# Two projections 512 columns wide, and layer 0's modulation multiplied unsplit in four column groups

## The chip, the cores and the metric

The kernel runs on one core of one Trainium2 chip. The metric is the device time of one execution in microseconds (us): the median of three runs is 1244.5 (1243.15 to 1247.92). The profile shows one execution more, with a span of 1242.4 us. Its engines are TensorE (PE; PEld is its weight load), VectorE (DVE), ScalarE (ACT), GpSimd (POOL) and SyncE (SP), which issues the loads.

## The reference

Two layers act on 512 prompt tokens and 256 sample tokens, which share the weights and have a modulation vector `c` each. The model width is 1024. For each layer:

```python
mod = jax.nn.silu(c) @ w_ada + b_ada
shift, scale, gate = jnp.split(mod, 3, axis=-1)
hid = _rms_norm(x, norm_g) * (1.0 + scale[:, None, :]) + shift[:, None, :]
qa, ka, va, za, qb, kb, vb, zb, ga, gb = jnp.split(hid @ w_in, split_at, axis=-1)
oa = _neighbourhood_attention(qa, ka, va, rpb)
qh = _axial_rope(_rms_norm(qb, q_norm_g))
kh = _axial_rope(_rms_norm(kb, k_norm_g))
ob = _gqa_attention(qh, kh, vb)
merged = sigmoid(ga) * ((oa * silu(za)) @ w_pa) + sigmoid(gb) * ((ob * silu(zb)) @ w_pb)
x = x + gate[:, None, :] * (merged @ w_out)
```

A final RMS norm ends the trunk. `va` are the values of the neighbourhood attention, `qb` the queries of the grouped attention; both are 512 columns wide and come from the same input `hid`.

## The kernel before, in words

**Numbers.** Every factor of a large product is held as a high and a low part in a rounded 32-bit format (fp32r), and a product is three: high x high, high x low, low x high. A weight of 128x1024 elements (512 KB, "half" or "unit") is loaded on SP into one of two buffers (`raw`, `w_load`), ScalarE rounds it (`whi`, L243), and VectorE, for five halves GpSimd, subtracts (`wlo`, L249). When `wlo` has been issued, `w_load` issues the next load but one, which waits on SP until its buffer is free; what stands behind it on SP waits too.

**Order.** All instructions are issued from one program in an order written out by hand. Main work is a list of steps (`step`), mostly of twelve products. Attention work comes as slots between the steps at a rate, and other pieces follow a number of steps later (`defer`). Each engine runs its instructions in the order of this program. At the start the order comes from a table instead: `put(t, fn)` with a written time `t`, sorted by it; `load` computes the times of the loads from their number and a cost `U`.

**The start.** The first work is the norm of the prompt's rows of x and layer 0's modulation. Sections 1 (scale) and 0 (shift) come as 16 quarters of 256 KB each (`adaraw`). A quarter is split by ScalarE (`adahi`) and by VectorE or GpSimd (`adalo`, L1051), three quarters stay unsplit; the matmuls `adap` multiply it with the silu of `c`, once for each group of tokens. Four quarters give 256 columns: `rows` copies the sums to SBUF, two small matmuls `adat` turn them into columns, and VectorE adds the bias to `ada_shift` or `ada_a`. From there come the eight parts k of the layer's input: VectorE multiplies x by `ada_a` and the norm `rb` (L285), ScalarE adds the shift and rounds (`hh`, L293), VectorE subtracts (`hl`, L299). Then va is multiplied: two chunks of 256 columns, the prompt's four token tiles of the first chunk with k outermost (each k starts when its `hh` and `hl` are there), then the second chunk, then the sample's two tiles, whose norm is computed meanwhile (`ssq`, `ssps`, `ms`, `ny`, `rb`). `acct` names these sums. Behind va come the "pairs" (`accp` for the prompt's 512 tokens, `accs` for the sample's 256): queries and keys of two heads, with the neighbourhood attention of the pair before in slots (`tp` transposes, `pth` and `ptl` copies in two parts, `op` and `os` products with the values).

**qb.** Two chunks of 256 columns, three sums of two token tiles each. Each sum is squared and copied by ScalarE (`rsq`, `rr`), reduced by VectorE (`qss`), and GpSimd multiplies by the rotary tables. When a chunk's three sums are through, `rope_finish` computes the reciprocal root of all 24 norms in twelve small VectorE operations and multiplies the three `rr` by it (L1314); TensorE transposes them (`qt`), ScalarE and VectorE copy these out (`GQ`). The chunk kvb and the slots of the last pair follow in the same way.

Of the kernel before, what the change touches and what calls it, by code (L numbers as in the profile page):

```python
# [7 lines left out]
F32 = mybir.dt.float32  # L8
# [17 lines left out]
    # the first loads: order of the quarters (section, chunk), where the rows of x and the first weights come in,  # L26
    # how early a load is issued, which engine takes the low part of a quarter (R: the quarter stays whole)
    ORD=((1, 0), (0, 0), (1, 1), (0, 1), (1, 2), (0, 2), (1, 3), (0, 3)),
    XB=0,
    XS=1,  # L30
    WAT=(9, 20),
    LA=7,
    PL0="VVGVGGGVVVRVGVVV",
    PL1="VRGGGVRVGVGVGVGV",
    GL=1.8,
    # the first products: allowances between the pieces of a quarter, a chunk and the layer's input
    ML0=0.5,
    ML1=0.5,
    RL0=0.5,
    RL1=1,  # L40
    FL=0.6,
    HL=1.5,
    PL=0.7,
    # the first norm: which engine adds a square (P: the tensor engine), allowances; products that keep the array's clock up
# [3 lines left out]
    WARM=(10, 1, 22, 0.73),  # L48
    CH=4,
    # pieces at which the next weights are split, and halves whose low part GpSimd takes  # L50
    AK0=(2, 5),
    AK1=(3, 5),
    PW=("wor01", "wor11", "va11"),
    # neighbourhood attention: steps before a pair's slots start, steps for 16 slots; steps for what is left of it
# [3 lines left out]
    # grouped attention: steps before its norms, transposes and slots, steps for the slots  # L58
    QF=6,
    QT=11,  # L60
    QTT=3,
# [4 lines left out]
    # the other modulation sections: steps for the slots, loads ahead, slots before the sums are added up  # L66
# [4 lines left out]
    # steps before the prompt's next input, and before its result  # L71
# [7 lines left out]
def trunk(ctx: ExitStack, tc: tile.TileContext, xT, wst, wad, wsd, vec, gain, trig, mask, eye, rpb, yT):  # L79
# [23 lines left out]
    cst = const.tile([128, 160], F32R, name="cst")  # L103
# [110 lines left out]

    chunk_of = {}
# [11 lines left out]
    def split_one(now=True):  # L227
        low_all()
        if done_split[0] >= len(splits):
            return  # L230
        name, k = splits[done_split[0]]
        i = done_split[0]
        w_load(i + 1)
        if k == 0:
            wts[name] = (
                wp.tile([128, 8, 256], F32R, tag="whi", name="whi"),
                wp.tile([128, 8, 256], F32R, tag="wlo", name="wlo"),
            )
        hi, lo = wts[name]
        r = raws.pop(i)  # L240
        rv = r.rearrange("p (k n) -> p k n", k=4)
        h = hi[:, 4 * k:4 * k + 4, :]
        A.activation(out=h, in_=rv, func=AF.Copy)  # L243
        done_split[0] += 1

        def low():
            key = f"{name[0]}{name[2] if len(name) > 2 else ''}{k}"
            eng = G if key in SC["PW"] and (name[1] or name[0] != "va") else V
            eng.tensor_sub(out=lo[:, 4 * k:4 * k + 4, :], in0=rv, in1=h.bitcast(F32))  # L249
            w_load(i + 3)  # L250

        lows.append(low)
        if now:
            low_all()
# [13 lines left out]
    def ahead(name, at):  # L268
# [35 lines left out]
    def hid_chain(l, g, xs):  # L304
        """Pieces that turn the finished rows of group g into the two parts of the layer's input."""
# [115 lines left out]
    def ada_rows(acc):  # L421
        rows = smp.tile([4, 256], F32, tag="rows", name="rows", bufs=1)
        A.activation(out=rows, in_=acc[0:4, :], func=AF.Copy)
        return rows

    def ada_col(rows):
        pt = ps_t.tile([128, 2, 2], F32, tag="t", name="adat")
        for m in range(2):
            mm(pt[:, m, :], rows[:, 128 * m:128 * m + 128], sel[0:4, :], m == 0, m == 1)
# [86 lines left out]
    def token_chunk(name, evac, banks=(0, 1, 2), kouter=False, keep=False, more=True):  # L516
        if not kouter:
            need_split(name)
        hi, lo = wts[name]
        if not keep:  # L520
            wts.pop(name)

        def mms(out, i, k, st):
            hh, hl = hid[i // 4, k]
            i = i % 4
            sl = slice(128 * i, 128 * i + 128)
            mm(out, hh[:, sl], hi[:, k, :], st, False)
            mm(out, hh[:, sl], lo[:, k, :], False, False)
            mm(out, hl[:, sl], hi[:, k, :], False, k == KC - 1)

        if kouter:
            accs = {b: ps_acc.tile([128, 2, 256], F32, tag="acc", name="acct") for b in banks}

            def piece(k):
                for b in banks:
                    for j in range(2):
                        mms(accs[b][:, j, :], 2 * b + j, k, k == 0 and j == 0)
                    if k == KC - 1:
                        evac(b, accs[b])
                if more and k in SC["AK1" if name[1] else "AK0"]:  # L540
                    ahead(name, k)

            return [lambda k=k: piece(k) for k in range(KC)]
        cur = {}
        for b in banks:
            for j in range(4):
                def f(b=b, j=j):
                    if j == 0:
                        cur[b] = ps_acc.tile([128, 2, 256], F32, tag="acc", name="acct")
                    i = 2 * b + j // 2  # L550
                    for k in range(4 * (j % 2), 4 * (j % 2) + 4):
                        mms(cur[b][:, j // 2, :], i, k, k == 0 and j == 0)
                    if j == 3:
                        defer(2, lambda: evac(b, cur[b]))
                    if more and (b == banks[0] and j == 2 or b == banks[1 % len(banks)] and j == (1 if len(banks) > 1 else 3)):
                        ahead(name, j)
                step(f)

    def feat_chunk(name, src, nk, evac, ksteps=2, groups=(0, 1), keep=False, sep=False):
        need_split(name)  # L560
        hi, lo = wts[name]
        if not keep:
            wts.pop(name)
# [3 lines left out]
        def mms(out, m, g, k, st):  # L567
# [3 lines left out]
            else:  # L571
                xh, xl = src[k]
                sl = slice(0, NP) if g == 0 else slice(NP, NT)
            ms = slice(128 * m, 128 * m + 128)
            mm(out, hi[:, k, ms], xh[:, sl], st, False)
            mm(out, hi[:, k, ms], xl[:, sl], False, False)
            mm(out, lo[:, k, ms], xh[:, sl], False, k == nk - 1)

        cnt = [0]
        for g in groups:  # L580
            for m in range(2):
                kk = per * (1 + g)
                for k0 in range(0, nk, kk):
                    def f(g=g, m=m, k0=k0, kk=kk):
                        if k0 == 0:
# [19 lines left out]
                        if not (keep and name[2] == 3) and cnt[0] in ((3, 6) if len(groups) == 2 else (3, 5) if groups[0] == 0 else (2, 3)):  # L605
                            ahead(name, k0)
                    step(f)

    v4s = {}

    def va_evac(l, i):
        nxt(("va", l, i))
        cell = {}

        def evv(b, acc):
            if not cell:
                cell[0] = vp.tile([128, 6, 4, 128], F32R, tag="v", name="v4")
                v4s[i] = cell[0]
            evac_v(cell[0], b, acc)
        return evv  # L620

    def evac_v(v4, b, acc):
        tiles = slice(2 * b, 2 * b + 2)
        vv = v4[:, tiles].rearrange("p t (r e) (u d) -> p (t r) (e u) d", e=2, u=2)
        base = v4[:, tiles]
        off = base.offset
        pp = pitch(base)
        hi_o = bass.AP(base.tensor, off, [pp, [256, 4], [192, 2], [1, 64]])
        lo_o = bass.AP(base.tensor, off + 64, [pp, [256, 4], [64, 2], [1, 64]])
        src = acc.rearrange("p t (r e d) -> p (t r) e d", e=2, d=64)  # L630
        A.activation(out=hi_o, in_=src, func=AF.Copy)
        defer(1, lambda: V.tensor_sub(out=lo_o, in0=src, in1=hi_o.bitcast(F32)))
# [340 lines left out]
    order = []  # L973
    for l in range(DEPTH):
        order += [("va", l, 0), ("va", l, 1)]
        order += [("pair", l, p) for p in range(4)]
        order += [("qb", l, 0), ("qb", l, 1), ("kvb", l)]
# [7 lines left out]
    for nm in order:  # L985
        plan_chunk(nm, 1 if nm[0] in ("pa", "pb") else 2)
# [6 lines left out]
    with tc.manual_schedule():  # L993
# [3 lines left out]
        V.memset(cst.bitcast(F32), 0.0)  # L997
        xs, x_s = x_tiles("x0")
# [5 lines left out]
        c4 = cst[:, 0:32].rearrange("p (k f) -> p k f", f=4)  # L1004
        csv = cs.rearrange("p (k g) -> p k g", g=2)
        V.tensor_copy(out=c4[:, :, 0:2], in_=csv)
        V.tensor_sub(out=c4[:, :, 2:4], in0=csv, in1=c4[:, :, 0:2].bitcast(F32))
# [3 lines left out]
        V.tensor_add(out=sel, in0=ident[:, 0:2], in1=ident[:, 2:4])  # L1011
# [14 lines left out]
        U = 0.73  # L1026
# [11 lines left out]
        def q_load(sec, k):  # L1038
            raw = galloc([128, 2, 256], F32, "adaraw")
            S.dma_start(out=raw, in_=wad[sec, k])  # L1040
            quarter[sec, k] = [raw]

        def q_hi(sec, k):
            h = galloc([128, 2, 256], F32R, "adahi")
            A.activation(out=h, in_=quarter[sec, k][0], func=AF.Copy)
            quarter[sec, k].append(h)

# [737 lines left out]
```

## Time and profile before

| what | us |
|---|---|
| median of three runs | 1244.5 |
| span of the profiled execution | 1242.4 |
| TensorE busy | 1217.4 (98%) |
| VectorE busy | 827.2 (67%) |
| ScalarE busy | 596.3 (48%) |
| GpSimd busy | 377.5 (30%) |
| first product of va starts | 27.25 |
| first product of a pair starts | 77.63 |
| va of layer 1: the last 204 products start | 652.36 |

Times in a view of the trace count from the start of the span. A row of the groups has the line, engine and operation, then out<-in, shapes and the count; behind the first bar the busy time in all and the mean of one in ns; behind the second the idle time ahead of them and what ended it. A row of a timeline has start, length, engine, line, names. Matmuls are pipelined: a product of 256 columns has a length of 0.28 us, though the next starts 0.12 us after it. A row of the windows has the stretch, its length, the busy time (and number) for PE, PEld, DVE, ACT and POOL, then the clock granted to TensorE (1.00 is full), the share of the DMA engines that was busy, and GB/s.

### The profile page before, as it was taken

What the parts mean: (1) busy time and instruction counts of PE and PEld (TensorE: products, weight loads), DVE (VectorE), ACT (ScalarE), POOL (GpSimd) and SP (SyncE); (2) the same over time, 40 slices, a digit from 0 to 9 for tenths busy, and PEclk for the clock granted to TensorE, in tenths of its full rate; (3) what the DMA queues carried; (4) which work ended last, traced back from release to release, by engine and by line L of the source; (5) the groups of instructions that cost most, each with busy time, mean ns of one, the idle gap of its engine ahead of it and who ended that gap; (6) DMA issues with size and microseconds to landing.
All of it is one profiled execution on the core that took longest, in us unless ns stands there. A gap on an engine that the chain in (4) does not pass through costs nothing.

```text
span 1242.4 us, 20757 instructions
## 1 busy us (share of the span) xinstructions
PE 1217.4 (98%) x7872; PEld 1099.6 (89%) x7872; DVE 827.2 (67%) x1610; ACT 596.3 (48%) x1246; POOL 377.5 (30%) x396
## 2 busy tenths in 40 slices
PE   8999999999999999999999999999999999999996
PEld 7999999989898988887899999998988998888886
DVE  6857787784556458998384678878556544773535
ACT  6546865555555432333243676655555542232323
POOL 5114446352222121111050354554322212211102
PEclk9999999999999999999999999999999999999998
DMA  9432331110011134555352333112011103331324
GB/s 356 132 108 74 91 108 35 64 41 34 34 52 51 55 105 143 173 178 192 127 181 72 91 94 91 52 52 69 18 52 52 47 22 103 121 116 52 127 94 153
DMA packets 48852, 118.38 MB, mean 95 GB/s; under 512 B 5488, under 2 KB 13040, under 8 KB 48752
## 3 DMA queue, kind: packets, MB, share of 16 engines
q1 hardware_dynamic: 48608, 116.98, 29.3%
q8 instruction: 62, 1.02, 0.3%
q14 instruction: 38, 0.31, 0.1%
q10 hardware_dynamic: 144, 0.07, 0.0%
HBM read 110.74 MB, written 6.29 MB: 94 GB/s over the span
## 4 chain that ended last, share of the span: by engine, by line
PE 77%; DVE 11%; ACT 3%; issue 3%; DMA 3%; POOL 2%; SPq 1%; DVEq 0%; ACTq 0%; POOLq 0%
PE accp L132 35%; PE accs L132 16%; PE acct L132 11%; DVE adaacc L455 4%; PE go L132 3%; PE gtp L918 3%; PE gsp L132 3%; DVE wlo L249 2%; DMA adaraw<-in_wad 2%; PE sp L132 1%; PE op L132 1%; ACT p L756 1%; PE tp L777 1%; POOL gp L907 1%; DVE adalo L464 1%
## 5 line engine op out<-in xcount | busy, mean ns | idle before, releaser
L132 PE MATMUL accp<-hh,whi 128*128 128x512 f32 x512 | 202.9, 396 | 0.0
L132 PE MATMUL accp<-hh,wlo 128*128 128x512 f32 x512 | 200.2, 391 | 2.1 <-DVE wlo L249 2.1
L132 PE MATMUL accp<-hl,whi 128*128 128x512 f32 x512 | 200.0, 391 | 0.0
L249 DVE TENSOR_TENSOR wlo<-raw,whi 128x1024 fp32r<-128x1024 f32 x119 | 158.0, 1329 | 8.6 <-ACT whi L243 7.8
L907 POOL TENSOR_TENSOR gp<-gp,gss 128x512 f32<-128x512 f32 x80 | 88.9, 1113 | 204.8 <-DVE gss L905 179.3
L132 PE MATMUL accs<-hh,whi 128*128 128x256 f32 x512 | 145.9, 285 | 0.0
L132 PE MATMUL accs<-hh,wlo 128*128 128x256 f32 x512 | 144.8, 283 | 0.0
L132 PE MATMUL accs<-hl,whi 128*128 128x256 f32 x512 | 144.7, 283 | 0.0
L132 PE MATMUL acct<-whi,hh 128*128 128x256 f32 x480 | 137.8, 287 | 0.0
L132 PE MATMUL acct<-whi,hl 128*128 128x256 f32 x480 | 135.9, 283 | 0.8 <-DVE hl L299 0.8
L132 PE MATMUL acct<-wlo,hh 128*128 128x256 f32 x480 | 135.8, 283 | 0.0
L243 ACT ACTIVATE whi<-raw 128x1024 fp32r<-128x1024 f32 x124 | 129.7, 1052 | 9.0 <-DMA raw<-in_wst 8.2
L132 PEld LDWEIGHTS accp<-hh,wlo 128*128 128x128 f32 x512 | 96.1, 188 | 24.5 <-DVE wlo L249 3.8
L132 PEld LDWEIGHTS accp<-hl,whi 128*128 128x128 f32 x512 | 96.4, 188 | 17.3
L132 PEld LDWEIGHTS accp<-hh,whi 128*128 128x128 f32 x512 | 96.3, 188 | 17.2
L132 PEld LDWEIGHTS accs<-hl,whi 128*128 128x128 f32 x512 | 97.9, 191 | 1.4
L132 PEld LDWEIGHTS accs<-hh,whi 128*128 128x128 f32 x512 | 97.8, 191 | 1.3
L132 PEld LDWEIGHTS accs<-hh,wlo 128*128 128x128 f32 x512 | 97.8, 191 | 0.0
L1498 POOL TENSOR_TENSOR th<-th 128x512 f32<-128x512 f32 (+1 forms) x32 | 43.5, 1371 | 171.1 <-DVE th L1491 171.1
L132 PEld LDWEIGHTS acct<-whi,hl 128*128 128x128 f32 x480 | 91.9, 191 | 1.2 <-DVE hl L299 1.0
L680 ACT ACTIVATE pth<-gtp 128x512 fp32r<-128x512 f32 x80 | 47.8, 597 | 92.8 <-PE go L132 73.1
L132 PEld LDWEIGHTS acct<-whi,hh 128*128 128x128 f32 x480 | 92.0, 192 | 0.0
(239 smaller groups left out, 3014.8 us busy)
## 6 DMA issues: line engine op xcount, KB each, us to landing
raw<-in_wst SPq DMA_DIRECT2D x124, 512.0 KB, 3.7
adaraw<-in_wsd SPq DMA_DIRECT2D x64, 256.0 KB, 3.0
adaraw<-in_wad SPq DMA_DIRECT2D x32, 256.0 KB, 5.9
u<-in_rpb SPq DMA_DIRECT2D x16, 354.5 KB, 5.2
u<-in_rpb SPq DMA_DIRECT2D x16, 236.5 KB, 4.7
out_y<-y SPq DMA_DIRECT2D x12, 256.0 KB, 2.9
x<-in_xT SPq DMA_DIRECT2D x8, 256.0 KB, 5.0
res<-in_xT SPq DMA_DIRECT2D x8, 256.0 KB, 3.3
```

The costliest lines, as they stand in the source:

```text
L132: T.matmul(out=out, lhsT=lhsT, rhs=rhs, start=start, stop=stop, skip_group_check=True)
L243: A.activation(out=h, in_=rv, func=AF.Copy)
L249: eng.tensor_sub(out=lo[:, 4 * k:4 * k + 4, :], in0=rv, in1=h.bitcast(F32))
L455: V.scalar_tensor_tensor(out=acc[n, h, g], in0=r, scalar=c, in1=acc[n, h, g], op0=ALU.mult, op1=ALU.add)
L464: V.tensor_sub(out=lo, in0=a, in1=hi.bitcast(F32))
L680: A.activation(out=h, in_=t, func=AF.Copy)
L756: A.activation(out=P[:, j, :], in_=P[:, j, :], func=AF.Exp, scale=-1.0, bias=ss[:, j:j + 1], accum_out=ss[:, 2 + j:3 + j])
L777: T.transpose(t[:, b, 128 * j:128 * j + 128], p_of(4 + j, b), ident)
L907: G.tensor_mul(out=pv_, in0=pv_, in1=ss[:, 4:4 + n].unsqueeze(2).to_broadcast([128, n, w]))
L918: T.transpose(t[:, q, 128 * j:128 * j + 128], src, ident)
L1498: G.tensor_add(out=t[:, sl], in0=t[:, sl], in1=mrg[k][:, sl])
```

## The change

**Width.** The weights of va and qb are laid out anew: four units of 128x1024, each two of the eight k, 512 columns wide. A product of these has 512 columns (`accw`) instead of two of 256 (`acct`), so that each projection of a layer has 144 products instead of 288. Weight parts are single units now, four buffers each. va takes the prompt's four token tiles with k outermost in four banks (`va_prompt`), then the sample's two in two banks of the transposes' pool (`va_sample`). qb runs over the token tiles (0, 1), (2), (3) and (4, 5) (`wide_pass`); squares, copies and rotary products come per token tile, and `rope_finish` comes twice: for tiles 0 to 3 (32 norms of a partition, four `rr`) and for 4 and 5 (16 norms, two `rr`). The prompt's transposes and the sample's have steps of their own.

**Modulation of layer 0.** Nothing is split any more: `adahi`, `adalo` and their ScalarE, VectorE and GpSimd work are gone at the start. Two quarters are multiplied together by four 32-bit products of 128x32 by 128x256, each on its own 32 columns of the array and into its own 32 rows of one bank; 16 such steps take the place of 32. `rows` copies all 128 rows, and `adat` adds the four groups up with a constant (`sel`).

**Loads.** First the eight rows of x, then four times: four quarters of section 1, four of section 0, one unit of va. Before, x rows and quarters alternated, and two halves of va came at the tenth and the twenty-first quarter. Then the sample's rows. The sample's squares, sums and norm have places in the table now: GpSimd adds all seven squares, before VectorE did.

The first place is TensorE's row in the start, near its end. `adap` are the modulation's products, `adat` turns its rows into columns, `acct` and `accw` are va. Before:

```order
L132 MATMUL adat<-sel,rows 128x2 x2
L132 MATMUL adap<-adahi,cst 128x256
L132 MATMUL adap<-adalo,cst 128x256
...
L132 MATMUL acct<-whi,hh_673 128x256
L132 MATMUL acct<-wlo,hh_673 128x256
L132 MATMUL acct<-whi,hl_674 128x256
...
L132 MATMUL adat<-sel,rows 128x2 x2
L132 MATMUL acct<-whi,hh_690 128x256
```

Now:

```order
L124 MATMUL adap<-adaraw,c_104 32x256 x4
L124 MATMUL accw<-whi,hh_521 128x512
...
L124 MATMUL adat<-sel,rows 128x2 x2
L124 MATMUL accw<-whi,hh_590 128x512
...
L124 MATMUL ssps<-ones,sq 128x1 x2
L124 MATMUL accw<-whi,hh_600 128x512
...
L124 MATMUL rb<-ident,ny 128x128 x2
L124 MATMUL accw<-whi,hh_674 128x512
```

A step of four products stands between six products of va, eleven of the sixteen behind the first `accw`. `ssps` of the sample stands between k=6 (`hh_590`) and k=7 (`hh_600`), and its `rb` directly ahead of its first products (`hh_674`).

The second place is VectorE's row in qb, where the first attention values of a step are split (`ptl`) and the norms are finished (`qss`, `ny`, `na`, `rr`). Before:

```order
L685 TENSOR_TENSOR ptl<-tp,pth 128x512
L761 RECIPROCAL ss<-ss 128x2
L764 TENSOR_SCALAR p<-p,ss 128x256 x2
L1308 TENSOR_SCALAR qss<-qss 128x24
L368 TENSOR_SCALAR ny<-qss 128x24
...
L1314 TENSOR_TENSOR rr<-rr,ny 128x512 x3
L1291 TENSOR_REDUCE qss<-rsq 128x8
```

Now:

```order
L237 TENSOR_TENSOR wlo<-raw,whi 128x1024 x2
L701 SCALAR_TENSOR_TENSOR oa<-os,otmp 64x256
L711 TENSOR_TENSOR ptl<-tp,pth 128x512
L1312 TENSOR_SCALAR qss<-qss 128x32
L367 TENSOR_SCALAR ny<-qss 128x32
...
L1317 TENSOR_TENSOR rr<-rr,ny 128x512 x4
L711 TENSOR_TENSOR ptl<-tp,pth 128x512
L1294 TENSOR_REDUCE qss<-rsq 128x8
```

The finish has four `rr` and stands between the two `ptl` of one `op`; before, it stood ahead of both (the `ptl` shown is that of the `os` before them). The core of the diff:

```diff
+    WIDE = dict(va=512, qb=512)
-        if k == 0:
-            wts[name] = (
-                wp.tile([128, 8, 256], F32R, tag="whi", name="whi"),
-                wp.tile([128, 8, 256], F32R, tag="wlo", name="wlo"),
-            )
+        hi = wp.tile([128, 1024], F32R, tag="whi", name="whi", bufs=4)
+        lo = wp.tile([128, 1024], F32R, tag="wlo", name="wlo", bufs=4)
...
-            w_load(i + 3)
+            if i > 1:
+                w_load(i + 3)
...
+    def token_mms(out, name, i, k):
+        hi, lo = part_of(name, k)
+        hh, hl = hid[i // 4, k]
+        sl = slice(128 * (i % 4), 128 * (i % 4) + 128)
+        mm(out, hh[:, sl], hi, k == 0, False)
+        mm(out, hh[:, sl], lo, False, False)
+        mm(out, hl[:, sl], hi, False, k == KC - 1)
...
+    def va_prompt(l):
...
+            for i in (2 * h, 2 * h + 1):
+                token_mms(accs[i], ("va", l), i, k)
+                if k == KC - 1:
+                    defer(1 + i % 2, lambda i=i: evac_v(i, accs[i]))
+        return [lambda k=k, h=h: piece(k, h) for k in range(KC) for h in range(2)]
+    def va_sample(l):
+        wide_pass(("va", l), [(4, 5)], evac_v, lambda i: ps_t.tile([128, NP], F32, tag="t", name="accw"), first=False)
...
         def q_mul(sec, k):
...
-                for n, part in enumerate(parts):
-                    mm(acc, cst[:, 4 * kc:4 * kc + 128], part[:, j, :], kc == 0 and n == 0, kc == KC - 1 and n == 1)
+            raw = [quarter.pop((sec, k - 1)), quarter.pop((sec, k))]
+            for g in range(4):
+                mm(acc[32 * g:32 * g + 32, :], c32[:, 2 * q - 2 + g, :], raw[g // 2][:, g % 2, :], q == 1, q == 3)
...
+        tx = [load(1, lambda k=k: load_x(0, k)) for k in range(KC)]
+        for i in range(4):
+            for sec in (1, 0):
+                ta[sec, i] = q_plan(sec, i)
+            tu[i] = load(2, lambda i=i: w_load(i + 1))
+        txs = [load(0.5, lambda k=k: load_x(1, k)) for k in range(KC)]
...
+        def sample_add(k):
+            if k == 0:
+                ssq[1] = sq.pop(0)
+            else:
+                G.tensor_add(out=ssq[1], in0=ssq[1], in1=sq[k])
+                gfree(sq.pop(k))
...
+            def q_evac(i, acc):
+                qr[i] = galloc([128, 1, 8, 64], F32, "rr")
+                rope_part(acc.rearrange("p (t h d) -> p t h d", t=1, d=64), tabs[0][:, i:i + 1], qr[i], qss[:, i:i + 1, :])
+                if i == 3:
+                    defer(SC["QF"], lambda: rope_finish([qr[t] for t in range(4)], qss[:, 0:4, :]))
+                    for pr in range(4):
+                        defer(SC["QT"] + SC["QTT"] * pr, lambda pr=pr: q_tr_p(pr))
+                if i == 5:
+                    defer(SC["QS"], lambda: rope_finish([qr[t] for t in (4, 5)], qss[:, 4:6, :]))
+                    for w in range(2):
+                        defer(SC["QST"] + SC["QTT"] * w, lambda w=w: q_tr_s(w))
...
+            wide_pass(("qb", l), [(0, 1), (2,), (3,), (4, 5)], q_evac,
+                      lambda i: ps_acc.tile([128, NP], F32, tag="acc", name="accw"))
```

More of the change, by code (lines that the diff above doesn't have):

```diff
@@ L266, in need_split, with need_unit, part_of, ahead @@
         low_all()
-    def ahead(name, at):
+    def need_unit(name, k):
+        while done_split[0] <= chunk_of[name][0] + k:
+            split_one()
+        low_all()
+    def part_of(name, k):
+        n = 1024 // WIDE.get(name[0], 256)
+        return [t.rearrange("p (k n) -> p k n", k=n)[:, k % n, :] for t in wts[name][k // n]]
+    def ahead(name):
         a, n = chunk_of[name]
@@ L513, in ada_side @@
         return out
[L516 to L543, printed above, removed]
+    def token_mms(out, name, i, k):
[5 more added lines that the diff above has]
+        mm(out, hl[:, sl], hi, False, k == KC - 1)
@@ L553, in f, with wide_pass @@
                     if j == 3:
                         defer(2, lambda: evac(b, cur[b]))
-                    if more and (b == banks[0] and j == 2 or b == banks[1 % len(banks)] and j == (1 if len(banks) > 1 else 3)):
-                        ahead(name, j)
+                    cnt[0] += 1
+                    if cnt[0] in (3, 6):
+                        ahead(name)
                 step(f)
+        wts.pop(name)
+    def wide_pass(name, groups, evac, alloc, first=True):
+        for n, tiles in enumerate(groups):
+            cur = {}
+            for q in range(4):
+                for j, i in enumerate(tiles):
+                    def f(q=q, j=j, i=i, n=n, tiles=tiles, cur=cur):
+                        need_unit(name, q)
+                        if q == 0:
+                            cur[i] = alloc(i)
+                        for k in (2 * q, 2 * q + 1):
+                            token_mms(cur[i], name, i, k)
+                        if q == 3:
+                            defer(2, lambda: evac(i, cur[i]))
+                        if j == len(tiles) - 1:
+                            if n == 0 and first and q < 2 and done_split[0] <= chunk_of[name][0] + q + 2:
+                                split_one(False)
+                                defer(1, low_all)
+                            if n == len(groups) - 1 and q < 3:
+                                ahead(name)
+                    step(f)
+        wts.pop(name)
@@ L605, in f @@
                         if not (keep and name[2] == 3) and cnt[0] in ((3, 6) if len(groups) == 2 else (3, 5) if groups[0] == 0 else (2, 3)):
-                            ahead(name, k0)
+                            ahead(name)
                     step(f)
+        if not keep:
+            wts.pop(name)
     v4s = {}
[L611 to L632, printed above, removed]
+    def evac_v(t, acc):
+        if not v4s:
+            for i in range(2):
+                v4s[i] = vp.tile([128, 6, 4, 128], F32R, tag="v", name="v4")
+        for i in range(2):
+            base = v4s[i][:, t]
+            pp = pitch(base)
+            hi_o = bass.AP(base.tensor, base.offset, [pp, [256, 2], [192, 2], [1, 64]])
+            lo_o = bass.AP(base.tensor, base.offset + 64, [pp, [256, 2], [64, 2], [1, 64]])
+            src = acc[:, 256 * i:256 * i + 256].rearrange("p (r e d) -> p r e d", e=2, d=64)
+            A.activation(out=hi_o, in_=src, func=AF.Copy)
+            defer(1, lambda lo_o=lo_o, src=src, hi_o=hi_o: V.tensor_sub(out=lo_o, in0=src, in1=hi_o.bitcast(F32)))
@@ new lines, in va_prompt, with piece @@
+    def va_prompt(l):
+        accs = {}
+        v4s.clear()
+        def piece(k, h):
+            need_unit(("va", l), k // 2)
+            if not accs:
+                for i in range(4):
+                    accs[i] = (ps_acc.tile([128, NP], F32, tag="acc", name="accw") if i < 3
+                               else ps_o.tile([128, NP], F32, tag="o", name="accw"))
+            for i in (2 * h, 2 * h + 1):
[3 more added lines that the diff above has]
+        return [lambda k=k, h=h: piece(k, h) for k in range(KC) for h in range(2)]
@@ L1345, in trunk @@
-            roping[0] = True
-            qb(0)
-            qb(1)
+                y = newton(ss.rearrange("p t h -> p (t h)"), n * nh).rearrange("p (t h) -> p t h", h=nh)
+                t = 0
+                for r in rs:
+                    k = r.shape[1]
+                    V.tensor_mul(out=r, in0=r, in1=y[:, t:t + k, :].unsqueeze(3).to_broadcast([128, k, nh, 64]))
+                    t += k
+            nxt(("qb", l))
+            roping[0] = True
+            qr = {}
+            qss = smp.tile([128, 6, 8], F32, tag="qss8", name="qss", bufs=1)
```

346 lines of the change are left out of this document (153 added, 193 removed).

## The prediction

> **What bounds the kernel now.** The page's table of busy time comes first, then the windows of the start, then the chain that ended last (start in us, length in us, what). These show whether a microsecond taken from TensorE is a microsecond of the span, and where not.
>
> ```profile
> PE 1217.4 (98%) x7872; PEld 1099.6 (89%) x7872; DVE 827.2 (67%) x1610; ACT 596.3 (48%) x1246; POOL 377.5 (30%) x396
> ```
> ```profile
> 0.00:5.00 5.00, 1.03 (x5) 1.03 (x6) 1.54 (x13) 2.13 (x3) 0.20 (x4) 1.00 0.60 165
> 5.00:10.00 5.00, 5.00 (x25) 3.93 (x25) 1.31 (x2) 3.75 (x6) 2.53 (x2) 1.00 1.05 395
> 10.00:15.00 5.00, 4.95 (x42) 4.73 (x42) 2.78 (x5) 4.50 (x9) 3.41 (x4) 1.00 1.06 390
> ...
> 30.00:35.00 5.00, 4.64 (x38) 4.42 (x38) 5.00 (x9) 1.84 (x4) 0.00 (x0) 1.00 0.92 315
> ```
> ```profile
> 61.80 15.83 PE acct L132 x132
> 77.63 10.91 PE accp L132 x48
> ```
>
> TensorE is busy 98% of the span, at the full granted clock (the 1.00 ahead of the DMA share). So its own instructions, not transfers, set the time nearly everywhere. The exception is the start. Until the first product of a pair (`accp`) at 77.63, TensorE runs modulation and va, VectorE is full (5.00 of 5.00) and transfers arrive at 390 GB/s. The questions are therefore how many TensorE microseconds the change removes, when the start is over, and whether VectorE or ScalarE, given other orders, now keep TensorE waiting. The last chain rows give two prices, start to start: 10.91/48 = 0.2273 us for a 512-column product, 15.83/132 = 0.1199 us for a 256-column one.
>
> **The change part by part, and its costs.**
>
> *Width.* Two products of 256 become one of 512: 2 x 0.1199 - 0.2273 = 0.0126 us saved. va and qb have 144 such pairs each in a layer, so 1.8 us a projection and 7.2 us in all, if TensorE then has no new wait.
>
> *Modulation of layer 0.* Before, a quarter is split by ScalarE and VectorE or GpSimd and multiplied in 0.12 us steps. Now four unsplit products of 32 columns, each on its own column group, form one step; there are 16 steps, 11 of them behind the first va product. The trace has unsplit products only on one column group, as two records each:
>
> ```profile
> 35.36 1.02 PE L132 MATMUL adap<-adaraw,csil 128*2 128x256 f32 x4
> 36.31 0.39 PE L132 MATMUL adap<-adahi,cst 128*128 128x256 f32 x1
> 36.54 0.28 PE L132 MATMUL adap<-adalo,cst 128*128 128x256 f32 x1
> 36.66 0.28 PE L132 MATMUL adap<-adahi,cst 128*128 128x256 f32 x1
> ```
>
> Four records take 0.95 us start to start, of which 0.10 is the switch of number format; the row behind is late by another 0.11 (0.23 instead of 0.12). A record is then 0.21, a pair of switches 0.21. Nothing in the trace shows two column groups at once, so I bound a step: all four side by side, two records and switches, 0.64 us; all in a row, eight records, 1.91. The quoted row stands at the upper end. Between lies: the second record of a product needs the same columns as the first, so only the next product's first record can run beside it. That is five record times, 1.27 us, and I take it, since it assumes parallel groups and an unchanged order of records.
>
> The Trainium skill has a rule on each side. TensorE: Matmul & The Clock Gate, Part 3 (Packing small matmuls), states a gain of 2.38 for three column tiles, and that products start and end in program order; if four tiles gain at least that, a step is 8 x 0.21 / 2.38 + 0.21 = 0.92 us, by this estimate 1243; the quoted rows agree with the order. TensorEngine Tiling (Array Packing), Key Properties, states that a change of tiling mode drains TensorE; a quoted product lasts 0.28 us but hands on after 0.12, so 22 drains of 0.16 would be 3.5 us more, by this estimate 1250.5 (rival D). No trace here shows column groups, so neither is borne out yet.
>
> *The first loads.* Eight rows of x, eight quarters and one 512 KB unit now come first: 18 x 0.262 = 4.7 MB. The windows above move 0.83 + 1.98 + 1.95 = 4.75 MB by 15 us, so the unit is there at 15. The queue on SP is reordered too: behind the third and fourth units' loads, which wait there for the `wlo` of the first and second (two raw buffers), stand the quarters of the next piece and the sample's x0s. They come later than the data rate allows, but TensorE, not they, is then the slower. Behind the unit's landing come:
>
> ```profile
> L249 DVE TENSOR_TENSOR wlo<-raw,whi 128x1024 fp32r<-128x1024 f32 x119 | 158.0, 1329 | 8.6 <-ACT whi L243 7.8
> L299 DVE SCALAR_TENSOR_TENSOR hl<-x,ada_shift,hh 128x512 fp32r<-128x512 f32 x8 | 6.9, 872 | 0.8 <-ACT hh L293 0.8
> L293 ACT ACTIVATE hh<-x,ada_shift 128x512 fp32r<-128x512 f32 x8 | 5.6, 713 | 5.6 <-DVE ada_shift L411 5.6
> L423 ACT ACTIVATE rows<-adap 4x256 f32<-4x256 f32 x8 | 2.9, 368 | 3.8 <-PE adap L132 3.8
> L411 DVE TENSOR_TENSOR ada_shift<-adat,vecs 128x4 f32<-128x4 f32 x4 | 0.6, 153 | 0.5 <-PE adat L132 0.5
> ```
> ```profile
> 44.90 0.60 PE L132 MATMUL adat<-sel,rows 4*128 4x2 f32 x4
> 45.43 0.39 PE L132 MATMUL adap<-adahi,cst 128*128 128x256 f32 x1
> ```
>
> Rows 0.37, the column products 0.53, shift 0.15, hh 0.71, and on VectorE wlo 1.33 and hl 0.87: 4.0 us, so 19.0; in TensorE's row stand five modulation steps, two `adat` and `rb` ahead, for which I add 1.5 (bounds -1 and +3): the first `accw` at 20.5.
>
> From there to the first `accp`: 96 prompt products, 21.8; 11 steps; six `adat` with their switches, 3.3; `ssps` and `rb`, 1.0; 48 sample products, 10.9; and waits. The waits: the last `adat` stands directly ahead of the products of k=6, so shift, wlo and hl (2.35 us, less two products that need no hl, 0.45) are open, 1.9. The two blocks before it hide most of the same under one step, 0.6 each, 1.2 together. The sample's norm follows:
>
> ```profile
> L357 POOL TENSOR_TENSOR ssq<-ssq,sq 128x256 f32<-128x256 f32 x7 | 9.5, 1352 | 59.0 <-ACT sq L355 57.2 <-DVE t L285 1.8
> L355 ACT ACTIVATE sq<-x0s 128x256 f32<-128x256 f32 x7 | 2.3, 406 | 0.0
> L285 DVE SCALAR_TENSOR_TENSOR t<-x0s,ada_a,rb 128x256 f32<-128x256 f32 x8 | 3.6, 475 | 0.5 <-PE rb L132 0.5
> L299 DVE SCALAR_TENSOR_TENSOR hl<-t,ada_shift,hh 128x256 fp32r<-128x256 f32 x16 | 7.3, 477 | 0.0
> L293 ACT ACTIVATE hh<-t,ada_shift 128x256 fp32r<-128x256 f32 x16 | 7.7, 506 | 5.7 <-DVE t L285 5.7
> ```
>
> Its squares now stand in ScalarE's row behind the last `rows` and `whi`; GpSimd's seven adds are 9.5 us at 1.35 each. `ssps` stands on TensorE between k=6 and k=7, and I let it wait 2.5. Behind `rb`, t, hh and hl of 0.475, 0.506 and 0.477 are open, 1.4. Together 7.0 (bounds 4 and 9.5; at the low end the adds are done early). Sum: 20.5 + 21.8 + 3.3 + 1.0 + 10.9 + 7.0 = 64.5, plus 11 x 1.27 = 14.0: 78.5 against 77.63, **+0.9**. It holds the width's gain in this va.
>
> *qb.* TensorE has no slack to lose there: 0.29 + 0.21 us idle in these 70 us, beside VectorE at 9.8 of 10 in one window.
>
> ```profile
> 175.00:185.00 10.00, 9.71 (x82) 9.51 (x81) 9.83 (x26) 6.49 (x18) 4.94 (x4) 1.00 0.30 99
> ...
> 205.00:215.00 10.00, 9.79 (x83) 9.62 (x82) 8.19 (x13) 5.80 (x11) 9.31 (x9) 1.00 0.16 54
> ...
> sum 70.00, PE 69.50 PEld 68.59 DVE 57.66 ACT 40.14 POOL 39.16; mean PE 9.93 PEld 9.80 DVE 8.24 ACT 5.73 POOL 5.59
> ```
> ```profile
> 198.41 0.67 DVE L685 TENSOR_TENSOR ptl<-tp,pth 128x512 fp32r<-128x512 f32 x1
> ...
> 199.72 0.17 DVE L1308 TENSOR_SCALAR qss<-qss 128x24 f32<-128x24 f32 x1
> ...
> 202.38 1.90 DVE L1314 TENSOR_TENSOR rr<-rr,ny 128x512 f32<-128x512 f32 x3
> 204.20 0.68 DVE L1291 TENSOR_REDUCE qss<-rsq 128x8 f32<-128x512 f32 x1
> ```
>
> A rope finish is twelve small operations, 202.38 - 199.72 = 2.66, and three `rr`, 1.82 (0.61 each). The new one for the prompt has four `rr`: 5.1 us in one piece. The order puts it between the two `ptl` of one attention step, and behind the second stands `op` on TensorE. From the transposes on, `pth` on ScalarE (0.60 by its row below), `ptl` 0.67, the finish 5.1 and the second `ptl` 0.67 are 7.0 us. TensorE has 24 products and half of `op`, 24 x 0.2273 + 4 x 0.12 = 5.9. The wait is 1.1 by that, and 3.2 if `whi` and a `wlo` get in ahead on the same queues (1.05 and 1.33, less what overlaps); I take 2.0. Everything behind `op` (the next transposes and kvb) waits with it.
>
> ```profile
> L680 ACT ACTIVATE pth<-tp 128x512 fp32r<-128x512 f32 x48 | 28.5, 599 | 5.9 <-PE tp L785 2.6 <-PE tp L788 2.1
> L243 ACT ACTIVATE whi<-raw 128x1024 fp32r<-128x1024 f32 x124 | 129.7, 1052 | 9.0 <-DMA raw<-in_wst 8.2
> ```
>
> The sample's finish (twelve small operations, two `rr`: 3.9 us, behind a `wlo` of 1.33) stands ahead of its transposes during kvb. It costs 0 if the 120 kvb products ahead of them, 14.4 us, cover it, and 3.6 if that `wlo` and GpSimd's last rotary products come late; I take 1.5, nearer the cover. Per layer -1.8 + 2.0 + 1.5 - 0.5 (the old idle time) = 1.2, both layers **+2.4**.
>
> *va of layer 1.* -1.8 for the width; four weight units are split inside it, each 1.05 + 1.33 us under 24 products of 5.5 us, and the sample's chain now runs between the steps of the prompt. Bounds 0 and 2, taken 1.0: **-0.8**. Four 128x512 banks take the place of two; evacuations are per token tile, the same columns in all, and hidden under the products that follow.
>
> The sum: 0.9 + 2.4 - 0.8 = +2.5 on the profiled execution's 1242.4 us, 1244.9. The median of the runs is 2.1 above that span; so **1247**, +0.2%. From no change about 0.5% (6.2 us) can be told: 1238.3 to 1250.7.
>
> **Rivals.** *A, the groups run wholly side by side.* A step is 0.64, the start ends at 64.5 + 7.0 = 71.5, so 7.0 us less than in the sum: 1240. For it: four different outputs, four different weights. Against: in the trace no record of TensorE ever starts with another. If the qb waits are at their low end too (1.1 and 0), it is 1235.
> *B, the groups run one after another.* A step is 1.91, the start ends at 85.5, 1254: slower. For it: the quoted unsplit rows do so. It decides from a step of 1.6 us on (11 x 0.33 = 3.6 brings 1250.7).
> *C, VectorE's row in qb.* The finish between the two `ptl` costs its upper 3.2, and the sample's 3.6; per layer +4.5 instead of +1.2, so 1253.6: slower. It decides from about 5.3 us of new wait per layer on; for it, VectorE at 9.8 of 10; against, that the old finish left TensorE 0.5 us idle.
> *D, the array runs empty at each change between whole-width products and column groups.* A quoted 128-row product ends 0.16 us after the next could start (0.28 - 0.12); twice at 11 steps, with the forecast's 1.27, is 1250.5. Against: the switch of format shows only 0.10.
>
> **How the numbers follow.** Forecast 0.30, A 0.34, B 0.15, C 0.15, D 0.06. By the bounds of its other terms 0.18 of the forecast is no change, 0.07 faster, 0.05 slower; of A 0.17 is faster, 0.16 no change, 0.01 slower; of B and C 0.22 is slower, 0.07 no change, 0.01 faster; of D 0.04 is slower, 0.02 no change. Faster 0.25, same 0.43, slower 0.32. The range is 1236 (A with nearly the low qb waits) to 1259 (B with most of C's wait); the forecast's own is 1241 to 1253.
>
> **What would show it.** The start-to-start time of one modulation step, four pairs of records: 1.27 or near 0.64 or 1.9. The first `accw` at 18 to 22 and the first `accp` at 76 to 81. The waits view: `ssps` behind GpSimd's add, `op` behind `ptl` near 2 us in each layer, `qt` behind `rr`. `accw` at 0.227. I am wrong if the start ends beyond these bounds, or if waits of more than 4 us stand in a place not named here.

## The result, and the profile after

The change makes the kernel slower: 1264.6 us, median of four runs, against 1244.7 before (four runs, with one more than the 1244.5 of the table); the ratio is 1.016, its 95% interval 1.0144 to 1.0177. The profiled execution has a span of 1261.5 us, 19.1 more than that of before. The prediction was 1247, within a range of 1236 to 1259. The time is outside.

First, the page of the changed kernel: busy times, and the row of the granted TensorE clock in 40 slices; then the same row of the kernel before.

```profile
PE 1222.2 (97%) x7301; PEld 1067.4 (85%) x7301; DVE 810.8 (64%) x1600; ACT 580.8 (46%) x1229; POOL 362.3 (29%) x391
...
PEclk9999998899999999999999999999999999999998
```
```profile
PEclk9999999999999999999999999999999999999998
```

TensorE has fewer instructions, but is busy for longer, and two slices have a lower clock. Before, no slice but the last had one. The windows, cut at the stages, tell where. First the kernel before, then the changed kernel (stretch, length, busy PE, PEld, DVE, ACT, POOL, the granted clock, DMA share, GB/s). The rows between, the pairs and the long rest of a layer, are left out.

```profile
27.00:77.00 50.00, 48.11 (x380) 45.70 (x380) 40.48 (x78) 26.50 (x51) 7.74 (x5) 1.00 0.36 122
...
166.00:233.00 67.00, 66.50 (x556) 65.97 (x555) 54.80 (x129) 37.98 (x88) 37.12 (x41) 1.00 0.18 57
...
640.00:677.00 37.00, 35.97 (x297) 35.52 (x297) 21.95 (x45) 13.06 (x22) 7.13 (x3) 1.00 0.25 81
...
765.00:832.00 67.00, 66.20 (x555) 65.71 (x555) 54.73 (x130) 37.68 (x87) 38.64 (x42) 1.00 0.19 57
```
```profile
24.00:76.00 52.00, 47.10 (x261) 32.25 (x260) 27.74 (x64) 20.67 (x43) 6.75 (x7) 0.97 0.41 139
...
165.00:244.00 79.00, 71.07 (x416) 63.77 (x415) 57.43 (x133) 38.20 (x87) 36.75 (x41) 0.91 0.16 49
...
651.00:688.00 37.00, 35.23 (x152) 28.68 (x152) 20.82 (x49) 13.57 (x26) 5.18 (x3) 0.95 0.29 92
...
777.00:852.00 75.00, 67.16 (x413) 59.61 (x412) 57.26 (x131) 37.96 (x86) 35.90 (x40) 0.98 0.18 51
```

The stages end at these products in the two timelines; the last column is the difference in what the stage takes. (The timeline has the first `accp` of before at 77.47; the 77.63 that the prediction goes by is the chain's.)

| stage | before, us | changed, us | difference |
|---|---|---|---|
| start, to the first `accp` | 77.5 | 76.2 | -1.3 |
| qb and kvb, layer 0 | 166.2 to 232.6 | 165.0 to 243.5 | +12.1 |
| va, layer 1 | 639.6 to 676.7 | 650.8 to 688.2 | +0.3 |
| qb and kvb, layer 1 | 765.4 to 832.1 | 777.0 to 852.1 | +8.5 |
| all other | | | -0.5 |

So the whole loss is made in qb, twice. The waits view of TensorE in the changed kernel names what it waited for (us in total, times, longest):

```profile
PE qt L1356 <- DVE rr L1317: 7.8, 2, 3.9
PE op L124 <- DVE ptl L711: 7.5, 4, 2.8
PE accw L124 <- ACT hh L292: 3.0, 4, 1.1
...
PE accw L124 <- DVE xn L1578: 1.8, 1, 1.8
...
PE kt L1396 <- DVE rr L1317: 1.2, 2, 0.6
```

The first two are qb's: 15.3 us in both layers, against 0.5 and 0.8 us idle in the rows of before. The last, at kvb's transposes `kt`, stands behind qb's stage, 0.6 in each layer. The chain of the changed kernel shows how the 2.8 came about, and the windows what followed:

```profile
203.63 1.07 ACT whi L231
204.72 1.23 DVE wlo L237
205.95 0.33 DVE oa L701
206.28 0.60 DVE ptl L711
...
209.53 2.50 DVE rr L1317 x4
212.02 0.61 DVE ptl L711
212.68 1.44 PE op L124 x5
214.12 0.85 PE tp L803 x4
214.97 2.56 PE acct L124 x12
...
238.72 4.63 PE acct L124 x24
```
```profile
209.00:212.00 3.00, 0.87 (x6) 0.59 (x4) 2.85 (x7) 0.29 (x1) 0.00 (x0) 0.98 0.01 3
212.00:218.00 6.00, 5.32 (x25) 5.32 (x26) 1.22 (x3) 0.00 (x0) 3.97 (x4) 0.50 0.01 3
...
233.00:237.00 4.00, 0.39 (x4) 0.19 (x2) 3.52 (x13) 0.00 (x0) 1.71 (x3) 0.85 0.42 131
237.00:243.00 6.00, 5.63 (x27) 5.37 (x28) 4.75 (x11) 1.78 (x5) 1.86 (x4) 0.53 0.01 3
```

`whi` and `wlo` go ahead, then one `ptl`, then the finish without a break (its twelve small operations lie between 206.8 and 209.5), then the second `ptl`. TensorE stands from 209.8 to 212.7. When it goes on, its clock is at 0.50 for six microseconds: twelve `acct` take 2.56 us, 0.21 each instead of 0.12. The same happens at the sample's transposes behind 3.9 us. A stretch costs what was busy in it times what was missing of the clock: 5.32 x 0.50 = 2.7 and 5.63 x 0.47 = 2.6, 5.3 in these rows of layer 0 (5.6 when they are cut at the edges of the lowered clock, which comes further down). In layer 1 only the second wait had this behind it:

```profile
822.00:825.00 3.00, 0.41 (x3) 0.41 (x4) 3.00 (x6) 0.00 (x0) 0.00 (x0) 1.00 0.01 3
825.00:828.00 3.00, 3.00 (x28) 3.00 (x28) 0.13 (x1) 0.20 (x1) 2.65 (x3) 1.00 0.02 5
...
846.00:850.00 4.00, 3.20 (x14) 2.96 (x15) 3.47 (x7) 0.95 (x3) 0.00 (x0) 0.59 0.01 4
```

### The profile page after: what moved, and what is told of

It is laid out like the page before. It is cut to its first block, busy times and chain, and to the rows that moved or that the text cites. A ratio compares the mean times of both kernels' runs of the same rounds, so it can differ in the third digit from the quotient of the medians.

```text
span 1261.5 us, 19544 instructions
## 1 busy us (share of the span) xinstructions
PE 1222.2 (97%) x7301; PEld 1067.4 (85%) x7301; DVE 810.8 (64%) x1600; ACT 580.8 (46%) x1229; POOL 362.3 (29%) x391
## 4 chain that ended last, share of the span: by engine, by line
PE 75%; DVE 14%; ACT 5%; issue 3%; POOL 2%; DMA 0%; DVEq 0%; ACTq 0%; POOLq 0%
PE accp L124 33%; PE accs L124 16%; PE accw L124 8%; PE go L124 3%; PE gtp L944 3%; DVE adaacc L454 3%; PE gsp L124 3%; DVE wlo L237 3%; PE acct L124 2%; ACT p L782 1%; PE sp L124 1%; PE junk L124 1%; PE op L124 1%; DVE ptl L711 1%; ACT whi L231 1%
## 5 line engine op out<-in xcount | busy, mean ns | idle before, releaser
L124 PEld LDWEIGHTS accp<-hh,whi 128*128 128x128 f32 x512 | 96.3, 188 | 17.6
L454 DVE SCALAR_TENSOR_TENSOR adaacc<-adaraw,csil,adaacc 128x512 f32<-128x512 f32 x112 | 86.6, 828 | 3.9 <-DMA adaraw<-in_wsd 3.9
L711 DVE TENSOR_TENSOR ptl<-gtp,pth 128x512 fp32r<-128x512 f32 x80 | 54.6, 685 | 47.3 <-ACT pth L706 47.3
L124 PE MATMUL accw<-whi,hh 128*128 128x512 f32 x192 | 79.2, 413 | 4.8 <-ACT hh L292 3.0
L124 PE MATMUL accw<-whi,hl 128*128 128x512 f32 x192 | 77.0, 401 | 1.1 <-DVE hl L298 1.1
L124 PE MATMUL accw<-wlo,hh 128*128 128x512 f32 x192 | 76.7, 399 | 0.0
```

What stands on the lines that cost most here:

```text
L124: T.matmul(out=out, lhsT=lhsT, rhs=rhs, start=start, stop=stop, skip_group_check=True)
L454: V.scalar_tensor_tensor(out=acc[n, h, g], in0=r, scalar=c, in1=acc[n, h, g], op0=ALU.mult, op1=ALU.add)
L711: V.tensor_sub(out=lo, in0=t, in1=h.bitcast(F32))
```

## The experiments

The theory to test was that the loss is VectorE's order in qb, made dearer by the clock. The rivals were that wide products, column groups or new loads cost elsewhere too; that VectorE has too much work in the wide form wherever it stands; and that the clock falls for another reason.

**qb as before, all else changed.**

```diff
-    WIDE = dict(va=512, qb=512)
+    WIDE = dict(va=512)
...
-            wide_pass(("qb", l), [(0, 1), (2,), (3,), (4, 5)], q_evac,
+            qb_chunk(0)
+            qb_chunk(1)
```

Its `QF`, `QT` and `QTT` have their old values again too, so this run doesn't part width from order.

> The change with qb alone as before: two chunks of 256 columns, one finish of 24 norms each. Everything else (wide va, column groups, loads) stays. Theory 1, the loss is made in qb: by the trace the changed kernel needs 78.5 and 75.2 us from the first product of qb to the first pair product behind kvb, before 66.4 and 66.7, so 20.6 us go and the time is 1244, the same as before. Theory 2, wide products, column groups or the new loads cost elsewhere as well: it stays above 1252.

Measured: 1244.7 us, the ratio to the kernel before 1.0003 (0.9986 to 1.0019). The loss is in qb, all of it. Wide va, column groups and loads together are worth nothing measurable.

**The finishes later.** Four numbers (the expectation counts five), no instruction more or less.

```diff
-    QF=5,
-    QT=8,
+    QF=7,
+    QT=11,
-    QS=6,
-    QST=9,
+    QS=7,
+    QST=13,
```

> The change with five numbers changed: the prompt's finish of the norms two steps later, its transposes three steps later, the sample's finish one step and its transposes four steps later. No instruction is added or taken away. Theory 1, VectorE's finish stands ahead of what TensorE needs next: the waits of 2.8 and 3.9 us in each layer go, with them the lowered clock behind them; 20.6 us and what the width saves in qb, 3.6, go less 1.6 for the shorter wait on ptl that stays, so 1242. Theory 2, VectorE has too much work in qb in the wide form, wherever it stands: the waits come back at other instructions and the time stays at 1255 to 1265.

Measured: 1247.0 us, ratio 1.0017 (1.0004 to 1.0031). Order alone gives back 17.6 us of the 20, so the amount of VectorE's work isn't the cause of these. The stage from qb's first product to the first `accp` takes 65.2 us in both layers, 1.2 and 1.5 less than before. But 1242 is missed by 5. In the waits of this kernel a new first row stands, from behind the stage:

```profile
PE kt L1396 <- DVE rr L1317: 5.1, 2, 2.5
...
PE op L124 <- DVE ptl L711: 1.9, 2, 1.0
```

`kt` are kvb's transposes. Behind the later finish of the sample, VectorE reaches kvb's finish 2.5 us too late, in each layer: 5.1 us where the changed kernel had 1.2, and in layer 1 the clock is at 0.50 behind it from 848.5 to 851.9, 1.6 more.

**Products in the wait.** Ahead of the sample's first transposes:

```diff
                 t = ps_t.tile([128, 2, NS], F32, tag="t", name="qt")
+                if w == 0:
+                    for _ in range(14):
+                        mm(t.rearrange("p a b -> p (a b)"), cst, cst.unsqueeze(1).to_broadcast([128, 4, 128]), True, True)
```

> The change with 14 products of 512 columns on constants ahead of the sample's first transposes of qb, in each layer; their sum is overwritten. They lie in the wait of 3.9 us and make it no shorter (14 x 0.227 = 3.2 us). Theory 1, TensorE standing still lowers the clock granted to it: the stretches at 0.50 behind these two waits (about 6.7 and 4 us, half of which is lost) go, 4.8 us less, 1260. Theory 2, the clock falls for another reason: 1264.6 or slower.

Measured: 1260.8 us, ratio to before 1.0119 (1.0093 to 1.0145): 3.8 less than the change, with 14 products more in each layer, near the first theory's 4.8. The profiled execution is the slowest of the five, 1268.2 (the others 1259.4 to 1261.3): in its start the clock is at 0.50 from 11.4 to 25.0, far ahead of the added products. The windows of its layer 0, the first holding the added products and the wait:

```profile
240.00:246.00 6.00, 5.08 (x29) 3.96 (x28) 5.49 (x16) 0.47 (x2) 2.80 (x3) 1.00 0.28 90
246.00:252.00 6.00, 6.00 (x42) 5.56 (x43) 4.12 (x9) 3.94 (x12) 2.36 (x4) 1.00 0.00 0
```

The clock stays at 1.00 where the change had 0.53. The transposes come no sooner for it, so TensorE's standing still is what lowers the clock there. Behind the first waits of the same execution, on `op`, to which nothing was added, it is lowered in both layers, from 223.0 and from 830.6.

**One column group instead of four.**

```diff
-                mm(acc[32 * g:32 * g + 32, :], c32[:, 2 * q - 2 + g, :], raw[g // 2][:, g % 2, :], q == 1, q == 3)
+                mm(acc[0:32, :], c32[:, 2 * q - 2 + g, :], raw[g // 2][:, g % 2, :], q == 1 and g == 0, q == 3 and g == 3)
```

> The change with the four products of a modulation step on one column group instead of four, summed in the same rows of the bank; rows copies 32 rows and adat sums 32. Theory 1, the groups run side by side: a step of 0.57 us becomes eight records of 0.21 and a switch, 1.8 to 1.9; eleven steps behind the first product of va make 14, of which about 2 go into waits that are there now, so the first pair product comes at 87 to 90 instead of 76.2 and the time is 1276 to 1279. Theory 2, the start is bound by loads and VectorE, the step's length hides: the first pair product before 80 and the time below 1269.

Measured: 1282.4 us, ratio 1.030 (1.028 to 1.0327), and the first `accp` at 95.0, later than either theory said. One step of this kernel, then one of the changed kernel, each with the product behind it:

```profile
37.97 1.91 PE L124 MATMUL adap<-adaraw,c 128*32 128x256 f32 x8
39.81 0.50 PE L124 MATMUL accw<-whi,hh 128*128 128x512 f32 x1
```
```profile
24.52 0.64 PE L124 MATMUL adap<-adaraw,c 128*32 128x256 f32 x8
25.09 0.50 PE L124 MATMUL accw<-whi,hh 128*128 128x512 f32 x1
25.43 0.39 PE L124 MATMUL accw<-wlo,hh 128*128 128x512 f32 x1
```

Eight records take 1.84 us on one group and 0.57 on four. The trace has the first records of the four products within 0.02 us of each other at 24.52, and the second records likewise 0.22 later: the groups run wholly side by side. The 1.27 us of difference make 14.0 at eleven steps, and the five steps ahead of the first `accw` bring it to 29.0 instead of 22.5; of these 20.5 us 18.7 arrive at the first `accp`.

**The start in another order.** In the changed kernel the last steps stand in TensorE's row behind products of va, up to 50 us, though their loads are there long before: by the timeline of SP the last eight quarters are issued by 30.9, and by the table of loads one lands 6.0 us after that.

```profile
25.17 5.68 SPq L1067 DMA_DIRECT2D adaraw<-in_wad  x8
```
```profile
adaraw<-in_wad SPq DMA_DIRECT2D x32, 256.0 KB, 6.0
```

First the steps alone, 2, 4 and 6 us earlier in the table:

```diff
-                t = load(1, lambda k=k: q_load(sec, k)) + SC["ML"]
+                t = load(1, lambda k=k: q_load(sec, k)) + SC["ML"] - (0, 2, 4, 6)[i]
```

> The change with only the modulation steps of pieces 1, 2 and 3 standing 2, 4 and 6 us earlier in the table of times; qb as changed. Theory 1, the order of the start costs it 4 to 6 us: the waits on hh and hl go with the lowered clock behind them, 1258 to 1261. Theory 2, loads or VectorE bind the start: 1264.6.

Measured: 1257.5 us, ratio to before 1.0116 (1.0103 to 1.0129), 7.1 less than the change. The first `accp` starts at 71.3. The stretch below has no lowered clock and 2.4 us idle; the changed kernel had 0.97 and 4.9 in as long a one. The 4.9 us at the first `accp` are the start's part of the 7.1; behind the first wait of layer 0's qb the clock is lowered for 3.4 us here (from 209.1) and for 6.8 in the changed kernel, which is 1.3 of the rest:

```profile
20.00:72.00 52.00, 49.56 (x299) 35.12 (x299) 31.46 (x70) 23.65 (x49) 5.57 (x7) 1.00 0.51 176
```

Then this order with VectorE adding the sample's squares, and the later finishes of qb, the sample's transposes one step earlier than above:

```diff
-                G.tensor_add(out=ssq[1], in0=ssq[1], in1=sq[k])
+                V.tensor_add(out=ssq[1], in0=ssq[1], in1=sq[k])
...
+    QST=12,
```

> finish_later, with the sample's transposes one step earlier than there, and the start in another order: in the table of times the modulation steps of pieces 1, 2 and 3 (with their rows, adat and what follows) stand 2, 4 and 6 us earlier, and VectorE adds the sample's squares. No work is added or removed. Theory 1, in the start TensorE waits for a chain that stands too late in the rows, though its loads landed by 38 us: the waits of 0.4, 0.4, 1.0 and 0.6 us on hh and hl, the 2.4 on GpSimd's adds and the lowered clock behind them (1.7) go, 6 us, and the first pair product comes at 69 to 72 instead of 76 to 80; with qb as in finish_later the time is 1238 to 1241, below the kernel before. Theory 2, the start is bound by the loads or by VectorE: the first pair product stays at 75 or later, the time at 1245 to 1247.

Measured: 1238.7 us, ratio 0.9973 (0.9957 to 0.9988), the first `accp` at 67.9. That is the first version below the kernel before. No stretch of its profiled execution has a lowered clock, but for the last 6 us.

**What follows qb.** Two runs moved the sample's transposes by one step.

```diff
-    QST=13,
+    QST=12,
```

> finish_later with one number changed: the sample's transposes one step earlier (12 instead of 13). In finish_later the wait went on to kt, 2.5 us in each layer, behind kvb's finish, ahead of which VectorE had eight copies of the sample's transposes. Theory 1, VectorE's row decides: the copies come about 1.4 us earlier, the wait on kt is 1 to 1.5 in each layer and the clock stays up behind it: 1243 to 1245. Theory 2, another engine (ScalarE's copies) holds kt: 1247 as before.

Measured against finish_later: 1249.1 us, ratio to before 1.0057 (1.004 to 1.0074): by the medians 2.1 slower and neither theory, though its four runs go from 1247.3 to 1254.6. `kt` waits as long as with step 13, and the transposes now wait for VectorE's copies too, 1.0 a layer:

```profile
PE kt L1396 <- DVE rr L1317: 4.9, 2, 2.5
...
PE qt L1356 <- DVE GQ L675: 2.0, 2, 1.0
```

> both_moved with the sample's transposes at step 13 as in finish_later. In both_moved TensorE waits 1.0 in each layer at these transposes for a bank of the transposes' pool that VectorE's copies have not yet freed, and 2.5 at kt. Theory 1: the 1.0 goes in each layer, kt's wait stays, 1236 to 1237.5. Theory 2, the two waits trade places: 1238 to 1240.

Measured: 1240.0 us, ratio 0.9966 (0.9951 to 0.9982), the same as both_moved within the intervals. The wait on `GQ` is gone (`kt` 2.6, `op` 1.0 a layer are left), but the profiled execution has a mean clock of 0.993, that of both_moved 0.998. What else holds kvb's finish back stays open; these two runs don't tell.

**Narrow qb in the better start.** The last question is what the wide qb is worth at all.

> narrow_qb (qb in two chunks of 256 columns as before) with the start in the order of both_moved. It tells what the wide form of qb is worth when nothing stands wrong: narrow_qb was 1244.7 with the first pair product at 78.3, both_moved has it at 67.9. Theory 1, the wide qb's 3.6 us are given back behind it (in both_moved the stage itself takes 65.2 us instead of 66.4, but what follows up to layer 1's va 411.2 instead of 407.0): narrow_moved is 1233 to 1236, below both_moved's 1238.7. Theory 2, the width pays: 1239 or more.

Measured: 1234.8 us, ratio 0.9924 (0.9904 to 0.9943): the fastest version, 4.0 below both_moved. From qb's first product to the next layer's va it takes 473.5 us (160.2 to 633.7), both_moved 476.4 (156.7 to 633.1). In the stage itself the wide form saves 1.1 (65.2 against 66.3), behind it it loses 4.0 (411.2 against 407.2). Of these, 2.5 are the wait at `kt` and 1.0 that of `qt` on `GQ`, neither of which narrow_moved has. So the waits for VectorE that the wide form leaves cost more than its width saves.

## Why the prediction was wrong, point by point

*Width, 0.0126 us a pair: right, where TensorE can go on.* With the finishes later the stage is 1.2 and 1.5 us shorter, near the 1.8. It was never the question.

*A modulation step, 1.27 us: wrong; rival A was right.* I let the second record of a product bar the next product's first. It does not: 0.57 us for all eight, measured. Against a stream of `accw`, a step costs 0.80: six `accw` with a step behind them take 1.59 us instead of 6 x 0.2273 = 1.36, so the switches around a step cost 0.37 (0.80 less two records of 0.216) and not 0.21. The Trainium skill gives 2.38 for three column tiles (TensorE: Matmul & The Clock Gate, Part 3). Four groups gain 1.84/0.57 = 3.2 here, with the switch inside, so 0.8 a group by both.

*The first `accp`, 78.5: inside its bounds (76 to 81) at 76.2, with wrong terms.* Steps at 0.80 take 5.2 us off. `accw` starts at 22.5 instead of 20.5, outside the bound of 22. The waits were 5.0 instead of 7.0 (4.1 on `hh` and `hl`, 0.9 on the adds), and a lowered clock from 54.9 to 58.3 added 3.17 x 0.50 = 1.6, which had no term. With these the sum is 78.5 - 5.2 + 2.0 - 2.0 + 1.6 = 74.9; 1.3 isn't resolved. What I took as given, that TensorE is the slower side there and the loads are through, was right; that its row order itself could be moved by 5 to 8 us was not seen.

*qb, +1.2 a layer: this is the step that failed.* Measured +12.1 and +8.5. Its mechanism is rival C's: the finish between two `ptl`, and the sample's finish ahead of its transposes. C's upper prices were 3.2 and 3.6; measured are 2.8 and 3.9, and 0.8 and 1.0 at an earlier `op`, which I hadn't named: 7.5 and 7.7 a layer instead of the 3.5 that I took. For the first wait I had written down that `whi` and `wlo` could go ahead, and then took a value near the middle. They did go ahead. For the second I argued by TensorE's cover of 14.4 us, but VectorE could not use it. By the chain it works from 229.4 to 237.8 with hardly a break, and the finish is the last of that:

```profile
229.36 0.68 DVE GQ L675
...
231.68 1.23 DVE wlo L237
232.90 0.36 DVE qss L1312
...
237.08 0.69 DVE rr L1317
237.82 0.90 PE qt L1356 x3
```

The cover on one engine says nothing about when the other gets to the work.

*The clock: no step at all.* I read 1.00 in every row and priced no wait by what it does to the clock. Here are lowered stretches of the changed kernel, cut at their edges: two of qb in layer 0, va's, and one of qb in layer 1. Ahead of the first and of va's stands the window before it.

```profile
208.47:211.88 3.41, 1.40 (x8) 1.04 (x6) 3.17 (x9) 0.82 (x2) 0.00 (x0) 1.00 0.09 35
211.88:218.70 6.82, 6.02 (x28) 6.02 (x29) 1.34 (x3) 0.28 (x1) 3.97 (x4) 0.50 0.01 2
...
235.77:242.59 6.82, 5.22 (x24) 4.96 (x25) 5.41 (x13) 1.78 (x5) 1.53 (x3) 0.50 0.02 7
...
652.20:655.61 3.41, 1.64 (x8) 1.25 (x8) 3.17 (x6) 1.90 (x3) 1.62 (x2) 1.00 0.90 314
655.61:659.02 3.41, 3.41 (x10) 2.63 (x9) 2.55 (x3) 1.97 (x3) 1.50 (x2) 0.50 0.35 99
...
846.75:850.17 3.42, 3.30 (x15) 3.02 (x16) 2.89 (x6) 1.11 (x4) 0.00 (x0) 0.50 0.02 5
```

Half of what was busy in them is lost: (6.02 + 5.22) x 0.50 = 5.6 us in layer 0 and 1.6 in layer 1 of qb, 1.7 in layer 1's va, and 1.6 in the start as above. With it rival C comes to -1.8 + 7.5 - 0.5 + 5.6 = 10.8 of 12.1 in layer 0 and -1.8 + 7.7 - 0.8 + 1.6 = 6.7 of 8.5 in layer 1; 1.3 and 1.8 aren't resolved.

The Trainium skill states the rule (TensorE: Matmul & The Clock Gate, Part 1): a window of about 3.4 us without work halves the clock, and a window of work restores it; the window runs free. The trace agrees on the half (0.50), on the length (each lowered stretch here lasts 3.41 us or twice that) and on the free run: the starts, 54.86, 211.88, 235.77, 655.61 and 846.75, lie 46, 7, 123 and 56 times 3.413 us apart. It does not agree that the window must be without work. TensorE was busy for 1.40 of the 3.41 us ahead of the first row that is lowered (0.41), for 0.48 of them in va, behind a wait of 1.8 us alone, and for 0.59 in the start. This is also how 2.8 us did it in layer 0 and not in layer 1: there the wait lies across two windows of the same grid, busy for 0.69 and 0.49. In all traces of this case, behind the first 25 us, every window at the full clock with less than 0.44 busy had a lowered one behind it (23 of 23); between 0.44 and 0.62 some had and some had not, and what decides there isn't shown.

*va of layer 1, -0.8: measured +0.3.* Without the 1.7 of its lowered stretch it is -1.4, inside the bounds.

*Rivals B and D* are out as they were priced. Four records that start together leave no room for groups in a row. And the changes cost less than D's 0.16: the first record of a step comes 0.32 us behind the last product (24.20 to 24.52) where 0.23 is usual, and the next product 0.31 behind the last record, as behind the unsplit product of before (36.01 to 36.31) and in same_group.

## What to carry to other kernels

On an engine that is 98% busy a wait can cost its length and then again 1.6 to 3 us, by the clock that is lowered behind it. The shortest single wait with a lowered clock behind it was 1.8 us here, and in the start waits of 1.4 us together did it; so price every new wait that can empty about half of a 3.4 us window with both. Before work is made coarser, look at what stands behind the coarser piece on the engine that does it: here waits and clock took 22.4 us in qb, the wide products there save 3.6 by their price, and four numbers of the order gave back 17.6. The rest of the coarser piece's cost stayed: with the better start, qb in 256 columns is 4.0 us faster than in 512. When a stage's loads are all there, the order of the rows is what bounds it: moving the modulation steps ahead brought the first `accp` from 76.2 to 71.3, and to 67.9 with VectorE adding the sample's squares, in an execution without a lowered clock in its start, and without any work less.

## What was not expected of the hardware

Four column groups multiply 32-bit operands wholly side by side, 0.57 us for four products of 128x32 by 128x256 with a switch, and 1.84 on one group. And the clock in the start differs between executions. narrow_moved and both_moved have the same start. In the profiled execution of the first, TensorE had 0.86 over the first 24 us, with 0.50 from 12.2 to 19.0, in that of the second 1.00. That alone is 3.2 us (22.63 x 0.14), and the first `accp` comes at 71.4 and at 67.9. So 3 us between two single executions say little about two kernels.

```profile
0.00:24.00 24.00, 22.63 (x122) 15.67 (x123) 6.99 (x33) 8.13 (x13) 2.79 (x6) 0.86 0.94 339
```
```profile
0.00:24.00 24.00, 22.49 (x149) 15.64 (x149) 9.76 (x39) 9.86 (x16) 2.77 (x6) 1.00 0.96 341
```

It isn't the standing still of qb: TensorE's records fill 3.23 of the 3.41 us ahead of this stretch. Its cause stays open. Nor does a row's 1.00 hold for the very first microseconds: in the changed kernel the products of 512 columns on constants start 0.43 us apart until 6.9, and 0.23 apart from 7.2 on.
